# Gate by chunk inside the scans, shared PSUM tiles in the second token block, and the output projection's loads between its weights

## The chip, the cores and the metric

The kernel runs on one core of a Trainium2 chip. The metric is the device time of one execution in microseconds. A core has five engines with queues of their own, each worked off in order: TensorE (PE, with its weight loads as PEld), VectorE (DVE), ScalarE (ACT), GpSimd (POOL) and SyncE (SP), whose queue issues most DMAs. ACT issues a few.

## What is computed

One layer of a diffusion backbone for 256 prompt tokens and 1024 sample tokens, width 1024, all in fp32. Cut to what matters here:

```python
h = rmsnorm(x, g_norm1) * (1.0 + scale_m) + shift_m
hc, gb, gc, z, xbc, dtf, dtb = jnp.split(h @ w_in, offs, axis=-1)
out_a = gb * dwconv1d(gc * hc, w_conv_short)
xbc = jax.nn.silu(dwconv1d(xbc, w_conv_ssd, b_conv_ssd))
y = y_f + y_b_rev[:, ::-1] + xh * d_skip[:, None]          # two scans, chunks of 128
y = rmsnorm(y * jax.nn.silu(z), g_ssd_norm)                # the gate, over 512 channels
x = x + gate_m * (jnp.concatenate([out_a, y], axis=-1) @ w_out)
h2 = rmsnorm(x, g_norm2) * (1.0 + scale_f) + shift_f
u = dwconv(h2 @ w_up)                                      # 3x3 on the sample, width 3 on the prompt
ug, uv = jnp.split(u, 2, axis=-1)
x = x + gate_f * ((jax.nn.silu(ug) * uv) @ w_down)         # then a final rmsnorm
```

## The kernel before

Channels lie on the 128 partitions, tokens along the free dimension. A product in fp32 is made of three matmuls with rounded parts: `wload` brings a weight tile into `raw`, ACT rounds it to `whi`, DVE or POOL subtracts to `wlo`, and `mm3` runs `whi` x hi, `whi` x lo, `wlo` x hi for each of the k tiles. A framework schedules the program: it traces the instructions, orders them for each engine by their place in the program and by when they are ready in a model of time, and sets the semaphores. `high_priority` moves what stands in it ahead. `after(a, b)` adds an edge that only orders.

The stages in order: the modulation and the first norm; `xbc`, the input projections of the scan; the scans; the gate; the output projection `wout` and the second norm; the feed-forward part in two token blocks (A: the prompt and 8 rows of the grid, B: the other 8 rows, 512 tokens), each of 22 pairs of `up` tiles (gate and value) with `down` tiles of the group before between them; a last norm.

**The scans.** The scan has a first pass, backward over the chunks (`ssd_pass1`), which stores a state for each chunk, and a second, forward (`ssd_pass2`), which makes the outputs. The prompt has 2 chunks, the sample 8. In the second pass a chunk takes two steps, one for each group of heads. A step takes one filler (`fill`), runs `output` (the matmuls into `yp`, then DVE adds them onto X) and, two steps ahead, `prep` (DVE adds the mask, ACT takes eight exponentials, DVE multiplies into `wm` and `csb`). The fillers are half projections of 24 matmuls that keep TensorE busy: the z projections of the sample (`zproj_halves`, 2 for each of 4 tiles, 8 in all) and the short convolution (`outa`, 6 for each of 4 tiles, 24 in all). The first pass over the sample takes one filler for each two chunks, the second pass 2, 2, 1, 1 over the prompt and 1 for each of 16 steps over the sample. What is left of the list runs after the scans.

**z and X.** `zproj_halves` copies z out of PSUM and ACT's queue stores it to DRAM (`zd`). X holds the scan's input and then its output: `xall` for the prompt, four tiles "xs" for the sample. `outa` stores its result as hi and lo to DRAM (`oad`).

**The gate** (lines 792 to 820) comes after both scans. For each token set it loads z, takes silu, multiplies it into X, squares on ACT, adds the four squares on DVE, sums over the partitions with a matmul against `ones` (L223), takes Ln and Exp on ACT for the reciprocal root (L226, L228), multiplies by gain and root, and splits the result into hi (ACT, L815) and lo (DVE) in the tiles `mya` (block A) and `myb` (block B). Before Ln a preload (L213) sets a table that holds Ln and Exp both.

**The output projection.** It loads `moa` (8 tiles of `oad`), `x1` (8 tiles of x) and `mob` (8 tiles) and then, in `wout`, for each of 8 tiles m the weights, `mm3` over `mya` and `moa`, and DVE adds onto `x1[m]`.

**PSUM.** From the output projection on there are three tiles "acc" of two banks each (`pacc2`) and two "dn" of one (`pdn`). In block B an `up` tile has 512 columns and fills one bank of an acc tile; a `down` tile has two parts of 288 columns, each in a dn.

Of the kernel before, what the change touches and what calls it, by code (L numbers as in the profile page):

```python
# [13 lines left out]
P = 128  # L14
# [41 lines left out]
def body(nc, tc, A):  # L56
    cnt = [0]

    def T(pool, shape, tag, bufs, dt=F32):
        cnt[0] += 1  # L60
        return pool.tile(list(shape), dt, tag=tag, bufs=bufs, name=f"{tag}_{cnt[0]}")
# [14 lines left out]
    def tt(out, a, b, op, eng=None):  # L76
        (eng or V).tensor_tensor(out=out, in0=a, in1=b, op=op)  # L77
# [17 lines left out]
    def smv(n):  # L95
        a, b = SMO[n]
        return sm[:, a:b]
# [174 lines left out]
    modv = mod.rearrange("p (b k) v -> p b k v", k=KT)  # L272
    badav = smv("bada").rearrange("p (b k) -> p b k", k=KT)

    def ada_block(k):
        wa = [T(xy, [P, 4, 2 * P], "xs", 4) for _ in range(2)]
        for i in range(2):
            dma(wa[i], A["w_ad1"][k, i])
        pm = psa()
        for j in range(KT):  # L280
            q = 32 * (j % 4)
            nc.tensor.matmul(pm[q:q + 32, 0:2 * P], sc[:, j, :], wa[j // 4][:, j % 4, :],
                             start=j < 4, stop=j >= 4, skip_group_check=True, tile_position=(0, q))
        s = T(cv, [P, 2 * P], "cv", 4)
        act(s, pm[:, 0:2 * P], AF.Copy)
        tp = pst()
        for b in range(2):
            nc.tensor.transpose(tp[:, b * P:(b + 1) * P], s[:, b * P:(b + 1) * P], ident)
        V.tensor_reduce(out=modv[:, 0:2, k],
                        in_=tp[:, 0:2 * P].rearrange("p (b g v) -> p b v g", b=2, g=4)[:, :, 0:2, :],  # L290
                        axis=mybir.AxisListType.X, op=ALU.add)
        tt(modv[:, 0:2, k], modv[:, 0:2, k], badav[:, 0:2, k].unsqueeze(2).broadcast_to([P, 2, 2]),
           ALU.add)
        ts(aff[:, 0, k], modv[:, 1, k], 1.0, smv("g1")[:, k:k + 1], ALU.add, ALU.mult)
# [55 lines left out]
        sets.append(s)  # L350
    SP, SS = sets
    oad = T(dr, [4, 2, P, TT], "oad", 1)
    zd = T(dr, [4, P, TT], "zd", 1)

    last_mm, mid_mm = [], [None]

# [44 lines left out]
    def zproj_halves(s, j, lo_eng):  # L401
        g = proj_halves(s, 12 + j, lo_eng)
        next(g)
        yield
        pp = next(g)
        z = T(cv, [P, s.T], "xl", 2)
        act(z, pp, AF.Copy)
        nc.scalar.dma_start(zd[j, :, s.t0:s.t0 + s.T], z)
        yield

    def outa(s, j, lo_eng):
# [170 lines left out]
            dma(st[0], A["st"][:, 1])  # L582
        return [(copies, step, c) for c in range(s.nc - 1, -1, -1)]

    def ssd_pass2(s, fill):


        sf = [None]
# [35 lines left out]
        def prep(u, g):  # L624
            csb = csbs[2 * u.c + g]
            wm = T(sw[0], [P, 8, L], "wm", 2)
            tt(wm.rearrange("p (a h) l -> p a h l", a=2), csb.rearrange("p (a h) l -> p a h l", a=2),
               s.mask.unsqueeze(2).broadcast_to([P, 2, 4, L]), ALU.add)
            for a in range(2):
                for h in range(4):  # L630
                    r = 32 * a + 4 * g + h
                    act(wm[:, a * 4 + h, :], wm[:, a * 4 + h, :], AF.Exp,
                        bias=s.tok[:, u.c, 0, r:r + 1])
            act(csb, csb, AF.Exp)
            tt(wm[:, 0:4, :], wm[:, 0:4, :], wm[:, 4:8, :], ALU.add)
# [33 lines left out]
        for i in range(2 * s.nc):  # L669
            behind = fill(s, i)  # L670
            if i % 2 == 1 and i + 1 < 2 * s.nc:
                u.step(behind)
            output(*us[i], behind)
            load(i + 3)
            if i + 2 < 2 * s.nc:
                if i % 2 == 0:
                    u = front(i // 2 + 1)
                us.append((u, i % 2))
                prep(*us[-1])
        if s.name == "p":  # L680
            dma(A["o_stf"], sf[0])

# [8 lines left out]
    SP.B, SP.C = bcp[0:2], bcp[2:4]  # L691
    SS.hi = lambda k: hs_hi[k]
    SS.lo = lambda k: hs_lo[k]
    SS.X = [T(xy, [P, TS], "xs", 4) for _ in range(4)]
    d4_s = dtcopy(SS, pd_s)
    for i in range(N_LOOP):
        xbc(SS, i, SS.X[i], PG)
# [58 lines left out]

    def fill(s, i):

        for _ in range(2 if s.name == "p" and i < 2 else 1):
            next(filler)  # L760
        return mid_mm[0]

# [3 lines left out]
    def steps(cps, behind):  # L766
        for (step, c, cp), b in zip(cps, behind):
            step(c, cp, b)
# [6 lines left out]
    for i in range(0, len(scan), 2):  # L775
        cps = pairs(scan[i:i + 2])
        next(filler)
        steps(cps, (mid_mm[0], last_mm[-1]))
    ssd_pass2(SP, fill)
    ssd_pass2(SS, fill)  # L780
    for _ in filler:
        pass
    close_pool(g_sw)
# [2 lines left out]

    g_ya, ya = open_pool("ya")
    g_yb, yb = open_pool("yb")
    g_gt, gt_ = open_pool("gt")
    mya = [[T(ya, [P, TA], "ya", 8, F32R) for _ in range(2)] for _ in range(4)]  # L790
    myb = [[T(yb, [P, OA], "yb", 8, F32R) for _ in range(2)] for _ in range(4)]
    def gate(s, behind):
        n = s.T
        acc = T(gt_, [P, n], "gq", 3)
        for j in range(4):
            z = T(gt_, [P, n], "gz", 2)
            dma(z, zd[j, :, s.t0:s.t0 + n])
            act(z, z, AF.Silu)
            tt(s.X[j], s.X[j], z, ALU.mult)
            if j == 0:  # L800
                act(acc, s.X[j], AF.Square)
            else:
                q = T(gt_, [P, n], "gq", 3)
                sq = act(q, s.X[j], AF.Square)
                tt(acc, acc, q, ALU.add)
        r = T(gt_, [P, n], "gq", 3)
        rstd(r, acc, n, pst, 512, sq, behind)
        for j in range(4):
            y = s.X[j]
            stt(y, y, smv("gsd")[:, j:j + 1], r, ALU.mult, ALU.mult)  # L810
            parts = [(0, n, mya, s.t0)] if s.name == "p" else \
                [(0, TA - TP, mya, TP), (TA - TP, TS, myb, 0)]
            for a, b, dst, o in parts:
                hi = dst[j][0][:, o:o + b - a]
                act(hi, y[:, a:b], AF.Copy)  # L815
                tt(dst[j][1][:, o:o + b - a], y[:, a:b], hi.bitcast(F32), ALU.subtract)
    with tc.high_priority():
        gate(SP, last_mm[-5])
        gate(SS, last_mm[-3])
    close_pool(g_xy)  # L820

    close_pool(g_gt)
    close_pool(g_cv)
    close_pool(g_hs)
    close_pool(g_ps)
# [10 lines left out]
        for i in range(2):  # L836
            dma(moa[j][i].bitcast(F32), oad[j, i, :, 0:TA])
    x1 = [T(x1p, [P, TT], "x1", 8) for _ in range(KT)]
    for k in range(KT):
        dma(x1[k], xT[:, k, :])  # L840
    mob = [[T(ob, [P, TB], "ob", 8, F32R) for _ in range(2)] for _ in range(4)]
    for j in range(4):
        for i in range(2):
            dma(mob[j][i].bitcast(F32), oad[j, i, :, TA:TT])

    def pacc2():
        return T(ps, [P, 1024], "acc", 3)
# [10 lines left out]
    def wout(src, parts, t0):  # L858
        for m in range(KT):
            wh, wl = wload(A["w_out"][m], PV)  # L860
            pp = pacc2()
            outs = []
            for c, a, b, v in parts:
                outs.append((pp[:, c:c + b - a],
                             (lambda k, a=a, b=b: src[k][0][:, a:b]),
                             (lambda k, a=a, b=b: src[k][1][:, a:b])))
            mm3(outs, wh, wl, KT)
            for c, a, b, v in parts:
                xx = x1[m][:, t0 + a:t0 + b]
                stt(xx, pp[:, c:c + b - a], col(2, m, v), xx, ALU.mult, ALU.add)  # L870
# [50 lines left out]
    def norm2_b_steps():  # L921
# [6 lines left out]

        return norm2_steps(TA, TB, [(0, 0, TB, 1)], alloc, done)

    def up(blk, m, h2s):
        wh, wl = wload(A["w_up"][m], PG)
        pp = pacc2()
        parts = PARTS_A if blk == 0 else PARTS_B
        outs = []
        for c, a, b, v in parts:
# [60 lines left out]
    def down(blk, gi, gs, ms):  # L997
        nj = GROUPS[gi]
        j0 = sum(GROUPS[:gi])
        t0 = 0 if blk == 0 else OA  # L1000
        for m in ms:
            raw = T(ff, [P, 4, P], "draw", 2)[:, 0:nj]
            off = (j0 * KT + m * nj) * P * P
            dma(raw, A["w_down"][off:off + nj * P * P].rearrange("(p j c) -> p j c", p=P, j=nj))
            wh = T(ff, [P, 4, P], "dhi", 2, F32R)[:, 0:nj]
            act(wh, raw, AF.Copy)  # L1006
            wl = T(ff, [P, 4, P], "dlo", 2, F32R)[:, 0:nj]
            tt(wl, raw, wh.bitcast(F32), ALU.subtract, PG)
            for a, b, v in DPARTS[blk]:
                o = pdn()[:, 0:b - a]  # L1010
                mm3([(o, (lambda k: gs[k][0][:, a:b]), (lambda k: gs[k][1][:, a:b]))], wh, wl, nj)
                xx = x1[m][:, t0 + a:t0 + b]
                stt(xx, o, col(5, m, v), xx, ALU.mult, ALU.add)
# [199 lines left out]
```

## Time and profile before

| what | us |
|---|---|
| median of the runs (3: 1585.49 to 1588.96) | 1585.58 |
| the profiled execution | 1583.09 |
| its span, first to last instruction | 1581.3 |
| mean granted TensorE clock | 0.991 |
| TensorE busy | 1521.7 |
| DVE busy | 1104.5 |
| ACT busy | 645.9 |
| POOL busy | 513.3 |

A row of the timeline names the start, the duration, the engine, the line, the operation, what it writes and what it reads, its shape, how often it stands there in a row, and in brackets the idle time before it with what ended it. A group row of the waits names who waited for whom, the sum in us, the times and the longest. The start times count from the first instruction. In this execution the second scan of the sample lies at about 345 to 463 us, the gate between 463 and 513, the output projection of block A starts at 512, and block B runs from about 1160 us.

### The profile page before, as it was taken

The page shows a single profiled execution, that of the slowest core. Times are in us where ns is not written, and L with a number is a line of the kernel's source. Part 1 is how long each engine was busy: PE and PEld are TensorE (multiplying, and loading weights), DVE is VectorE, ACT ScalarE, POOL GpSimd, SP SyncE. Part 2 cuts the span into 40 slices and gives each one's busy share as a digit, 9 for nine tenths or more (in the row PEclk, how much of TensorE's full clock was granted, in tenths as well). Part 3 has the DMA queues.
Part 4 walks back from the last instruction along what each step waited for, and adds up shares of the span by engine and source line. Part 5 has one row for each costly group of instructions (what it writes and reads, how often), then busy time and mean ns, then how long its engine had stood idle before and what let it go on. Part 6 is the DMA issues. An engine that isn't in the chain of part 4 may idle for free. (4 is left out here: it accounts for less than half of the span.)

```text
span 1581.3 us, 22424 instructions
## 1 busy us (share of the span) xinstructions
PE 1521.7 (96%) x8692; PEld 1293.7 (82%) x8692; DVE 1104.5 (70%) x1629; ACT 645.9 (41%) x1004; POOL 513.3 (32%) x288
## 2 busy tenths in 40 slices
PE   6988999999997999999999999999999999999997
PEld 3688667888785788888888888898888888888886
DVE  5765626376857339797666598656679878798696
ACT  6553434356557125433333353332334433433333
POOL 1445001111110000433333333333346555445452
PEclk9999999999998999999999999999999999999999
DMA  8555554333323712322222233212253333343221
GB/s 303 213 187 167 209 207 153 126 128 133 127 106 126 298 64 84 100 74 81 65 66 65 72 131 109 79 59 75 72 184 99 102 96 100 107 160 97 93 79 61
DMA packets 81756, 191.98 MB, mean 121 GB/s; under 512 B 9298, under 2 KB 31474, under 8 KB 81650
## 3 DMA queue, kind: packets, MB, share of 16 engines
q1 hardware_dynamic: 79922, 187.41, 34.7%
q10 hardware_dynamic: 1728, 3.15, 0.5%
q8 instruction: 68, 1.11, 0.3%
q14 instruction: 38, 0.31, 0.1%
HBM read 167.37 MB, written 23.15 MB: 120 GB/s over the span
## 5 line engine op out<-in xcount | busy, mean ns | idle before, releaser
L80 DVE SCALAR_TENSOR_TENSOR cc<-acc,sm,cc 128x504 f32<-128x504 f32 (+5 forms) x836 | 546.2, 665 | 110.7 <-ACT cc L953 52.4
L77 POOL TENSOR_TENSOR wlo<-raw,whi 128x1024 fp32r<-128x1024 f32 (+2 forms) x83 | 192.6, 2321 | 680.1 <-ACT whi L151 418.9
L151 ACT ACTIVATE whi<-raw 128x1024 fp32r<-128x1024 f32 x90 | 95.1, 1057 | 215.7 <-PE acc L162 186.4
L80 DVE SCALAR_TENSOR_TENSOR x<-dn,mod,x 128x288 f32<-128x288 f32 (+2 forms) x176 | 96.3, 547 | 93.8 <-PE dn L164 93.3
L77 POOL TENSOR_TENSOR dlo<-draw,dhi 128x512 fp32r<-128x512 f32 (+1 forms) x88 | 108.8, 1237 | 88.5 <-ACT dhi L1006 88.4
L160 PE MATMUL acc<-ya,whi 128*128 128x512 f32 (+1 forms) x400 | 120.9, 360 | 11.5 <-ACT yb L815 8.4
L164 PE MATMUL acc<-ya,wlo 128*128 128x512 f32 (+1 forms) x400 | 120.6, 359 | 0.3 <-DVE wlo L77 0.3
L162 PE MATMUL acc<-ya,whi 128*128 128x512 f32 (+1 forms) x400 | 120.6, 359 | 0.0
L164 PE MATMUL acc<-oa,wlo 128*128 128x512 f32 (+1 forms) x400 | 119.0, 355 | 0.0
L162 PE MATMUL acc<-oa,whi 128*128 128x512 f32 (+1 forms) x400 | 118.8, 354 | 0.0
L160 PE MATMUL acc<-oa,whi 128*128 128x512 f32 (+1 forms) x400 | 118.3, 353 | 0.0
L160 PE MATMUL dn<-yb,dhi 128*128 128x288 f32 (+2 forms) x352 | 109.5, 311 | 5.3 <-DVE x L80 4.1
L77 POOL TENSOR_TENSOR wlx<-raw,whx 128x1024 fp32r<-128x1024 f32 (+2 forms) x32 | 74.0, 2312 | 119.3 <-ACT whx L151 104.6
L162 PE MATMUL dn<-yb,dhi 128*128 128x288 f32 (+2 forms) x352 | 109.0, 310 | 0.8 <-POOL yb L77 0.8
L164 PE MATMUL dn<-yb,dlo 128*128 128x288 f32 (+2 forms) x352 | 109.0, 310 | 0.0
L160 PE MATMUL acc<-h,whi 128*128 128x512 f32 x320 | 105.0, 407 | 1.2 <-ACT whi L151 1.2
L164 PE MATMUL acc<-h,wlo 128*128 128x512 f32 x320 | 100.8, 396 | 1.8 <-POOL wlo L77 1.8
L1006 ACT ACTIVATE dhi<-draw 128x512 fp32r<-128x512 f32 (+1 forms) x88 | 52.9, 602 | 120.6 <-PE dn L162 50.1
L162 PE MATMUL acc<-h,whi 128*128 128x512 f32 x320 | 101.6, 396 | 0.0
L160 PE MATMUL dn<-g,dhi 128*128 128x288 f32 (+2 forms) x304 | 95.2, 314 | 0.0
L162 PE MATMUL dn<-g,dhi 128*128 128x288 f32 (+2 forms) x304 | 94.8, 312 | 0.3 <-POOL g L77 0.3
L160 PEld LDWEIGHTS acc<-ya,whi 128*128 128x128 f32 x400 | 76.5, 192 | 22.6 <-ACT yb L815 8.8
(343 smaller groups left out, 3624.0 us busy)
## 6 DMA issues: line engine op xcount, KB each, us to landing
raw<-in_w_up SPq DMA_DIRECT2D x88, 512.0 KB, 3.2
x<-in_w_ada SPq DMA_DIRECT2D x32, 512.0 KB, 5.4
draw<-in_w_down SPq DMA_DIRECT2D x64, 256.0 KB, 2.6
x<-in_w_in SPq DMA_DIRECT2D x24, 512.0 KB, 3.4
raw<-in_w_in SPq DMA_DIRECT2D x22, 512.0 KB, 6.9
xs<-in_w_ad SPq DMA_DIRECT2D x16, 512.0 KB, 8.4
csb<-csds SPq DMA_DIRECT2D x16, 512.0 KB, 4.3
raw<-in_w_out SPq DMA_DIRECT2D x16, 512.0 KB, 3.3
```

The source lines that it names most:

```text
L77: (eng or V).tensor_tensor(out=out, in0=a, in1=b, op=op)
L80: V.scalar_tensor_tensor(out=out, in0=a, scalar=s, in1=b, op0=op0, op1=op1)
L151: act(hi, raw, AF.Copy)
L160: nc.tensor.matmul(o, wh[:, k, :], rh(k), start=k == 0, stop=False)
L162: nc.tensor.matmul(o, wh[:, k, :], rl(k), start=False, stop=False)
L164: mm = nc.tensor.matmul(o, wl[:, k, :], rh(k), start=False, stop=k == n - 1)
L1006: act(wh, raw, AF.Copy)
```

## The change

- The four tiles of X of the sample become one tile `xq`, of which `ada_block` uses quarters for its weights as it used the tiles before.
- `zd` is laid out by chunk. For the sample silu is taken as z leaves PSUM; the prompt's z is copied and gets its silu in the gate.
- The first pass over the sample takes two fillers for each two chunks, the second pass over the prompt 2, 1, 1, 1.
- `gate` is a generator of three parts: load z; multiply, square, add the squares of channels 0, 1 to those of 2, 3; two matmuls against `ones`, Ln, Exp, multiply by the root. It runs for the whole prompt and for each chunk of the sample, called behind the steps of the second pass by `post_p` and `post_s`. Its z is a tile "cv", of which there are four for this and for `outa`. There is no preload of a table. The last chunk's last part is behind the scan.
- Behind the scans the gain is multiplied as the tiles are split: ACT scales and rounds to hi, DVE makes lo.
- `wout` loads `x1[m]` and one tile of `mob` behind each weight tile, and the loads ahead of it are gone.
- In block B the gate and value tile of a pair share one acc tile, a bank each, and every odd `down` tile takes an acc tile for its two parts.

```diff
+    xq = T(xy, [P, 4, TS], "xs", 1)
-        wa = [T(xy, [P, 4, 2 * P], "xs", 4) for _ in range(2)]
+        wa = [xq[:, 2 * (k % 2) + i].rearrange("p (j c) -> p j c", j=4) for i in range(2)]
...
-    zd = T(dr, [4, P, TT], "zd", 1)
+    zd = T(dr, [TT // L, P, 4, L], "zd", 1)
...
-        act(z, pp, AF.Copy)
-        nc.scalar.dma_start(zd[j, :, s.t0:s.t0 + s.T], z)
+        act(z, pp, AF.Silu if s.name == "s" else AF.Copy)
+        nc.scalar.dma_start(zd[s.t0 // L:s.t0 // L + s.nc, :, j].rearrange("c p l -> p c l"),
+                            z.rearrange("p (c l) -> p c l", l=L))
...
                 prep(*us[-1])
+            post(i)
...
-        for _ in range(2 if s.name == "p" and i < 2 else 1):
+        for _ in range(2 if s.name == "p" and i == 0 else 1):
             next(filler)
...
         cps = pairs(scan[i:i + 2])
         next(filler)
-        steps(cps, (mid_mm[0], last_mm[-1]))
-    ssd_pass2(SP, fill)
-    ssd_pass2(SS, fill)
+        mid_mm[0] = last_mm[-1]
+        next(filler)
+        steps(cps, (last_mm[-2], last_mm[-1]))
+
+    def gate(x, c0, n):
+
+        z = T(cv, [P, 4, n], "cv", 4)
+        for c in range(n // L):
+            dma(z[:, :, c * L:(c + 1) * L], zd[c0 + c])
+        yield
+        if c0 == 0:
+            act(z, z, AF.Silu)
+        tt(x, x, z, ALU.mult)
+        act(z, x, AF.Square)
+        tt(z[:, 0:2], z[:, 0:2], z[:, 2:4], ALU.add)
+        yield
+        pp = psa()
+        for i in range(2):
+            mm = nc.tensor.matmul(pp[:, 0:n], ones, z[:, i], start=i == 0, stop=i == 1)
+            if i == 0:
+                after(mm, last_mm[-1])
+        r = z[:, 2]
+        act(r, pp[:, 0:n], AF.Ln, scale=1.0 / 512, bias=epsc)
+        act(r, r, AF.Exp, scale=-0.5)
+        tt(x, x, r.unsqueeze(1).broadcast_to([P, 4, n]), ALU.mult)
+        yield
+
+    gate_p = gate(xall, 0, TP)
+    gates = [gate(xq[:, :, c * L:(c + 1) * L], SP.nc + c, L) for c in range(SS.nc)]
+
+    def post_p(i):
+        if i == 2 * SP.nc - 1:
+            next(gate_p)
+
+    def post_s(i):
+
+        c = i // 2
+        if i == 0:
+            next(gate_p)
+            next(gates[0])
+        if i == 1:
+            next(gate_p)
+        if i % 2 == 1:
+            next(gates[c])
+        else:
+            if c > 0:
+                next(gates[c - 1])
+            if c + 1 < SS.nc:
+                next(gates[c + 1])
+
+    ssd_pass2(SP, fill, post_p)
+    ssd_pass2(SS, fill, post_s)
+    with tc.high_priority():
+        next(gates[-1])
     for _ in filler:
         pass
...
     with tc.high_priority():
-        gate(SP, last_mm[-5])
-        gate(SS, last_mm[-3])
+        for x, dst, o in ((xall, mya, 0), (xq[:, :, 0:TA - TP], mya, TP), (xq[:, :, TA - TP:], myb, 0)):
+            n = x.shape[2]
+            for j in range(4):
+                g = smv("gsd")[:, j:j + 1]
+                hi, lo = [t[:, o:o + n] for t in dst[j]]
+                act(hi, x[:, j], AF.Copy, scale=g)
+                stt(lo, x[:, j], g, hi.bitcast(F32), ALU.mult, ALU.subtract)
...
-    for k in range(KT):
-        dma(x1[k], xT[:, k, :])
...
-    for j in range(4):
-        for i in range(2):
-            dma(mob[j][i].bitcast(F32), oad[j, i, :, TA:TT])
...
             wh, wl = wload(A["w_out"][m], PV)
+            if t0 == 0:
+                dma(x1[m], xT[:, m, :])
+                dma(mob[m // 2][m % 2].bitcast(F32), oad[m // 2, m % 2, :, TA:TT])
...
-        pp = pacc2()
+        if blk == 0:
+            pp = pacc2()
+        elif m < N_FF:
+            pair[0] = pacc2()
+            pp = pair[0][:, 0:512]
+        else:
+            pp = pair[0][:, 512:1024]
...
-            for a, b, v in DPARTS[blk]:
-                o = pdn()[:, 0:b - a]
+            both = pacc2() if blk == 1 and m % 2 else None
+            for i, (a, b, v) in enumerate(DPARTS[blk]):
+                o = (pdn() if both is None else both[:, 512 * i:512 * i + 512])[:, 0:b - a]
```

More of the change, by code (lines that the diff above doesn't have):

```diff
@@ L583, in ssd_pass1, with ssd_pass2 @@
         return [(copies, step, c) for c in range(s.nc - 1, -1, -1)]
-    def ssd_pass2(s, fill):
+    def ssd_pass2(s, fill, post):
         sf = [None]
@@ L693, in body @@
     SS.lo = lambda k: hs_lo[k]
-    SS.X = [T(xy, [P, TS], "xs", 4) for _ in range(4)]
+    SS.X = [xq[:, i] for i in range(4)]
     d4_s = dtcopy(SS, pd_s)
@@ L788, in body @@
     g_yb, yb = open_pool("yb")
-    g_gt, gt_ = open_pool("gt")
     mya = [[T(ya, [P, TA], "ya", 8, F32R) for _ in range(2)] for _ in range(4)]
     myb = [[T(yb, [P, OA], "yb", 8, F32R) for _ in range(2)] for _ in range(4)]
-    def gate(s, behind):
-        n = s.T
-        acc = T(gt_, [P, n], "gq", 3)
-        for j in range(4):
[L796 to L816, printed above, removed]
-    with tc.high_priority():
-        gate(SP, last_mm[-5])
-        gate(SS, last_mm[-3])
+    with tc.high_priority():
+        for x, dst, o in ((xall, mya, 0), (xq[:, :, 0:TA - TP], mya, TP), (xq[:, :, TA - TP:], myb, 0)):
[5 more added lines that the diff above has]
+                stt(lo, x[:, j], g, hi.bitcast(F32), ALU.mult, ALU.subtract)
     close_pool(g_xy)
-    close_pool(g_gt)
     close_pool(g_cv)
@@ L838, in body @@
     x1 = [T(x1p, [P, TT], "x1", 8) for _ in range(KT)]
-    for k in range(KT):
-        dma(x1[k], xT[:, k, :])
     mob = [[T(ob, [P, TB], "ob", 8, F32R) for _ in range(2)] for _ in range(4)]
-    for j in range(4):
-        for i in range(2):
-            dma(mob[j][i].bitcast(F32), oad[j, i, :, TA:TT])
     def pacc2():
@@ L929, in norm2_b_steps @@
         return norm2_steps(TA, TB, [(0, 0, TB, 1)], alloc, done)
+    pair = [None]
     def up(blk, m, h2s):
         wh, wl = wload(A["w_up"][m], PG)
-        pp = pacc2()
+        if blk == 0:
[5 more added lines that the diff above has]
+            pp = pair[0][:, 512:1024]
         parts = PARTS_A if blk == 0 else PARTS_B
```

## The prediction

> **What bounds the kernel now.** I read the totals first, then busy time by stretches of the span, then TensorE's waits, then the timeline where they cluster.
>
> ```profile
> PE 1521.7 (96%) x8692; PEld 1293.7 (82%) x8692; DVE 1104.5 (70%) x1629; ACT 645.9 (41%) x1004; POOL 513.3 (32%) x288
> 320.00:480.00 160.00, 158.76 (x1007) 129.37 (x1006) 113.05 (x148) 91.17 (x195) 21.92 (x9) 1.00 0.34 119
> 480.00:560.00 80.00, 65.25 (x303) 53.16 (x302) 43.07 (x49) 31.06 (x39) 2.89 (x1) 0.89 0.57 210
> 1280.00:1320.00 40.00, 40.00 (x226) 35.71 (x225) 32.34 (x55) 14.00 (x20) 22.34 (x13) 1.00 0.31 96
> ```
>
> In the stretches the columns after the length are the busy time of PE, PEld, DVE, ACT and POOL, then granted clock, DMA share and GB/s. TensorE is the bound: 158.8 of 160 us in the second scan, all of a stretch of the second token block. The hole is between scans and output projection: 65.3 of 80 us, at a clock of 0.89. Who left TensorE waiting from 200 to 560 us:
>
> ```profile
> PE acc L160 <- ACT yb L815: 8.4, 1, 8.4
> PE acc L160 <- ACT whi L151: 4.3, 2, 3.1
> PE acc L164 <- POOL wlo L77: 1.8, 1, 1.8
> PE sa L532 <- DVE xd L77: 1.3, 1, 1.3
> PE acc L164 <- DVE wlo L77: 0.3, 1, 0.3
> ```
>
> 8.4 us are the gate itself: the first matmul of the output projection waits for the last split tile that `gate` writes. The waits for whi and wlo are weight conversions: one pair stands behind the gate's work on ACT, the other (3.1 us) is a weight of the output projection and begins on SP's queue:
>
> ```profile
> 518.50 6.99 SPq L840 DMA_DIRECT2D x<-in_xT  x8
> 530.18 27.11 SPq L149 DMA_DIRECT2D raw<-in_w_out  x6
> 541.97 0.84 ACT L880 ACTIVATE nq<-x 128x768 f32<-128x768 f32 x1 [7.62 <-DVE x L80]
> 542.72 1.99 ACT L151 ACTIVATE whi<-raw 128x1024 fp32r<-128x1024 f32 x2
> 543.81 0.62 PE L160 MATMUL acc<-ya,whi 128*128 128x256 f32 x2 [3.06 <-ACT whi L151]
> ```
>
> Eight loads of x1 are issued ahead of six weight loads. The late weights are converted on ACT only behind a square of x1, which itself waited 7.6 us for the tile before; so it is the load's place in the order that costs. Behind each hole TensorE also runs slowly:
>
> ```profile
> 512.47 0.98 PE L160 MATMUL acc<-ya,whi 128*128 128x256 f32 x2 [8.40 <-ACT yb L815]
> 518.34 0.52 PE L160 MATMUL acc<-ya,whi 128*128 128x256 f32 x2
> 518.70 0.52 PE L162 MATMUL acc<-ya,whi 128*128 128x256 f32 x2
> 545.07 0.61 PE L164 MATMUL acc<-ya,wlo 128*128 128x256 f32 x2 [0.29 <-DVE wlo L77]
> 549.16 0.52 PE L160 MATMUL acc<-ya,whi 128*128 128x256 f32 x2
> 490.78 0.86 PE L160 MATMUL acc<-h,whi 128*128 128x512 f32 x2
> 494.65 0.62 PE L164 MATMUL acc<-h,wlo 128*128 128x512 f32 x2
> 464.79 0.62 PE L160 MATMUL acc<-h,whi 128*128 128x512 f32 x2
> 470.29 0.62 PE L160 MATMUL acc<-h,whi 128*128 128x512 f32 x2
> ```
>
> A row pair of the output projection takes 0.36 us (518.34 to 518.70). The nine from 512.47 to 518.34 took 5.87 instead of 3.2: 2.7 lost. From 545.07 to 549.16 are seven pairs, 4.1 instead of 2.5: 1.6 lost. A pair of the input projection takes 0.46 us (twelve rows from 464.79 to 470.29, which is one half projection, **5.5 us**); the five pairs from 490.78 to 494.65 took 3.87 instead of 2.3: 1.6 lost. **The stage loses** 8.4 + 4.3 + 1.8 + 0.3 + 2.7 + 1.6 + 1.6 = **20.7 us**.
>
> **The change, part by part.** *The holes.* After the change the gate of each chunk runs inside the scan. What stays behind the last output is one chunk's gate and the splits into mya and myb, twelve on ACT and twelve on DVE. Unit rows:
>
> ```profile
> 508.49 0.61 ACT L815 ACTIVATE yb<-xs 128x512 fp32r<-128x512 f32 x1
> 487.08 0.40 ACT L815 ACTIVATE ya<-xp 128x256 fp32r<-128x256 f32 x1
> 512.24 0.69 DVE L77 TENSOR_TENSOR ya<-xs,ya 128x512 fp32r<-128x512 f32 x1
> 468.39 0.43 DVE L77 TENSOR_TENSOR gq<-gq,gq 128x256 f32<-128x256 f32 x1 [0.51 <-ACT gq L804]
> ```
>
> Splits: ACT 4 × 0.40 + 8 × 0.61 = 6.5 us, DVE 4 × 0.43 + 8 × 0.69 = 7.2 us. Fillers: the list has 32 half projections. Before, the scans use 4 + 6 + 16 and 6 are left; after, 8 + 5 + 16, so 3 are left: 16.5 us of matmuls behind the last output. They cover 6.5 and 7.2 us, a gate of 4.0 (below), and the remaining short-convolution work. Only the last split of outa, its store and its reload come after the cover; four of eight k steps of the first output tile need mya alone, some 12 × 0.36 = 4.3 us of matmuls, and three accumulators let further tiles begin. I leave **3 us** (0 to 6): the 1.8 of a POOL conversion, plus 1.2 for the reload. The loads one by one take the 3.1 us wait and its 1.6 of slow rows away, since a weight then waits for one x1 and one mob at most; if that failed, these 4.7 would stay. Net: −20.7 + 3 = **−17.7**.
>
> *More TensorE work.* The sum over channels goes through the ones matrix in two halves, so twice the columns.
>
> ```profile
> 474.41 0.59 PE L223 MATMUL yp<-gq,ones 128*128 128x256 f32 x2
> 474.65 0.82 PE L160 MATMUL acc<-h,whi 128*128 128x512 f32 x2
> 475.31 0.62 PE L162 MATMUL acc<-h,whi 128*128 128x512 f32 x2
> 448.43 0.74 PE L160 MATMUL acc<-h,whi 128*128 128x512 f32 x2
> 455.86 0.74 PE L160 MATMUL acc<-h,whi 128*128 128x512 f32 x2
> ```
>
> 256 columns move the next pairs from 474.41 to 475.31, 0.9 instead of 0.46: 0.44 us. Before: 256 + 1024 columns, 2.2 us; after 4.4. Eight small groups break the stream; the 0.74 against 0.62 in the first pair after a scan output is 0.12 each, up to 0.2 with the issue before it. **+3.8** (2.2 to 5).
>
> *The scan.* A step is 7.43 us (448.43 to 455.86), a chunk 14.86. Per chunk DVE is busy 113.05/160 of that, 10.5 us, and ACT 91.17/160, 8.5 us. The gate adds:
>
> ```profile
> 919.60 1.28 ACT L226 ACT_TABLE_LOAD   x1
> 921.60 1.28 ACT L228 ACT_TABLE_LOAD   x1
> 475.53 0.47 ACT L226 ACTIVATE gq<-yp,epsc 128x256 f32<-128x256 f32 x1
> 476.01 1.28 ACT L798 ACT_TABLE_LOAD   x1
> 479.68 0.42 ACT L228 ACTIVATE gq<-gq 128x256 f32<-128x256 f32 x1
> ```
>
> Without the explicit preload, Ln loads a table and Exp loads another (919.60, 921.60); I take two loads for each of nine gates. ACT per chunk: 2 × 1.28 + 0.61 (square) + at most 0.47 and 0.42 = 4.0; DVE 0.69 + 0.43 + 0.69 = 1.8. So ACT goes to 12.5 and DVE to 12.3 of 14.86, both under TensorE. Behind a late Ln on ACT stand the exponentials of the mask of two steps on; DVE waits for those, and TensorE's output for DVE. The wm tiles are prepared two steps ahead, which leaves the chain a chunk. The before has no such gate in a scan; bounds: nothing, if the spare 2.4 us of ACT and 2.6 of DVE absorb it (a gain is excluded, nothing is taken out of the second scan), and 4.0 × 9 = 36 if every gate's ACT time stood bare. The nearest row is the 1.3 us that TensorE waited for xd, a tile handed over late once; 0.5 per gate gives **+4** (0 to 12). The prompt's silu on ACT, a table load and back, lies in this. The z loads are new on SP's queue in the scan; one waits for a cv tile until an older gate or outa has let go of it, and behind it stand the csb three steps on and the next w_in. They have two steps of cover, and the DMA share of the scan is 0.34, so I take 0 for them and for the store of z in pieces of 128 tokens; without the cover it is a step's wait, in the 12.
>
> The Trainium skill ("ScalarE: Activation LUTs", What ACT_TABLE_LOAD costs) speaks against this part: a switch costs about 2.66 us, 1.28 for the load and 1.38 of drain. The trace disagrees: the Ln at 475.53 ends at 476.00, and the load starts at 476.01. By the rule ACT would have 8.5 + 4.0 + 2 × 1.38 = 15.3 us in a chunk of 14.86 and the sum would be some 3 us worse, as an estimate.
>
> *The first scan* over the sample gets two half projections per two chunks in place of one. The xd wait of 1.3 lies there and a second half covers it: **−1** (−1.3 to +2, as z's silu can alternate tables with the exponentials).
>
> *PSUM of the second block.* TensorE's longest wait from 1080 us on, and the stretch in which it falls:
>
> ```profile
> PE dn L160 <- DVE x L80: 1.4, 1, 1.4
> 1400.00:1440.00 40.00, 37.41 (x215) 33.23 (x214) 39.17 (x59) 12.15 (x17) 18.93 (x11) 1.00 0.39 128
> ```
>
> DVE is busy 39.2 of 40 us there, and TensorE waits 1.4 for a down tile's bank. More banks let DVE fall behind without stopping TensorE, so the 1.4 goes. A pair holds its tile through both convolutions and an odd down tile takes one of the same three, so a wait can come instead. **−1.4** (−2.6, all that TensorE lacks in that stretch, to +4, three new waits of that kind).
>
> **Sum:** −17.7 + 3.8 + 4 − 1 − 1.4 = **−12.3**. The profiled execution took 1583.1 us (span 1581.3 and 1.8 around it), so 1570.8; the median of the runs is 2.5 higher, 1585.6, which gives **1573.3**. Instructions of ada_block only change how their tile is named: 0.
>
> **Rivals.** A row of today's gate bears on the second of them:
>
> ```profile
> 498.99 0.69 ACT L226 ACTIVATE gq<-yp,epsc 128x512 f32<-128x512 f32 x1 [2.76 <-PE yp L223]
> ```
>
> 1. *The scan takes back most.* DVE and ACT work in order and wait for each other; at 83% each a gate can cost TensorE 1.5 us, 9 × 1.5 = 13.5 in place of 4. For it: each gate has one chain DVE, ACT, TensorE, ACT, DVE. Against: 1.2 us idle in 160 today. 1583.
> 2. *Slower: Ln holds ACT.* The ones matmul is tied behind the end of the newest half projection. If Ln stands at ACT's head while that half still runs, ACT stops for up to 5.5 us per gate: 8.5 + 4.0 + 5.5 = 18.0 against 14.86, and the scan runs at ACT's pace, 3.1 × 8 = 25 in place of 4. It decides once the wait passes 2.4 us. For it: in the row, ACT stands 2.8 us before the ones matmul. Against: the squares are ready a step earlier, so the matmul is early if Ln is placed after it. 1573.3 + 21 = 1594.
>
> 3. *The hole only shrinks.* The last chunk's gate, splits, convolution and weight conversions meet on DVE and ACT as they do now; 3 becomes 11.7 (half of the 8.4 wait, the 2.7 of slow rows and a second POOL wait of 1.8 more): 1582.
> 4. *The loads change nothing.* An x1 load waits for memory and holds the next weights on the in-order queue: the 4.7 stays, 1578.
>
> **Chances.** Forecast 0.62 (1565 to 1578), rival 1 0.12, rival 2 0.09, rival 3 0.07, rival 4 0.06, better than all this (no new stall, no hole, 1562) 0.04. A measurement of this kernel can tell 0.3%, 4.8 us. Faster by more than that (under 1580.8): forecast, rival 4, the better case and some of 1 and 3: 0.77. Within: 0.13. Slower: 0.10. The range leaves out rival 2 and the far better end: **1562 to 1585**.
>
> **What would show it.** Right: no wait of TensorE over 2 us between the last scan output and the second output tile; no rows at 0.65 us a pair there; 18 more table loads in the scan, with TensorE above 97% busy; no wait for a w_out weight. Wrong: a step longer than 7.9 us, with TensorE's output waiting for DVE's wm or csb (rival 1), or Ln waiting over 2.4 us for the ones matmul (rival 2); an output projection that starts after a gap for ya or oa (rival 3); new waits of the second block for a cc.

## The result and the profile after

The changed kernel takes 1646.98 us (median of 6 runs, 1639.9 to 1652.04); the kernel before, beside it, 1586.39 (6 runs, 1584.27 to 1591.11). The ratio is **1.0375** (95% interval 1.0344 to 1.0405): slower by some 60 us, where 12 us less were forecast and the range ended at 1585. The profiled execution took 1646.87 us. One execution of experiment 5 below took 2510.5 us at a granted clock of 0.557 (without it that experiment's median is 1578.91 us), and the ratios compare the others.

The page of the changed kernel, its first line and the totals:

```profile
span 1645.1 us, 22507 instructions
PE 1545.9 (94%) x8722; PEld 1308.5 (80%) x8722; DVE 1092.8 (66%) x1634; ACT 661.2 (40%) x1025; POOL 514.3 (31%) x288
```

TensorE has 30 matmuls more than before (8722 against 8692) and is busy for 24 us more, yet for a smaller share of the span; no other engine has grown by much. The same stretches as before the change, in the same columns, and then all of the second token block (block B):

```profile
320.00:480.00 160.00, 153.86 (x987) 124.49 (x986) 124.49 (x165) 114.50 (x228) 23.15 (x9) 1.00 0.39 131
480.00:560.00 80.00, 74.05 (x417) 62.15 (x416) 40.57 (x53) 33.88 (x48) 2.41 (x1) 1.00 0.54 200
1280.00:1320.00 40.00, 35.60 (x182) 30.39 (x183) 22.69 (x40) 10.03 (x14) 14.18 (x9) 0.92 0.18 60
1400.00:1440.00 40.00, 32.66 (x154) 26.90 (x153) 27.78 (x43) 15.57 (x21) 14.06 (x9) 0.87 0.39 138
1160.00:1645.00 485.00, 428.81 (x2234) 371.24 (x2234) 338.04 (x557) 156.71 (x227) 208.10 (x128) 0.94 0.26 85
```

The last row against the same work in the kernel before:

```profile
1165.00:1581.00 416.00, 402.99 (x2234) 356.54 (x2234) 346.45 (x557) 156.80 (x227) 207.78 (x128) 0.99 0.30 99
```

The second scan lost some 5 us of TensorE time (158.76 to 153.86), the hole behind it got back 9 (65.25 to 74.05, at full clock). Block B begins 5 us earlier, at 1160 in place of 1165, and then runs 485 us in place of 416, with the same 2234 matmuls, 557 instructions of DVE's and 227 of ACT's. Of these 69 us TensorE stands idle for 43.2 (485.00 − 428.81 against 416.00 − 402.99), and 25.8 are the same matmuls at a lower granted clock (428.81 − 402.99; 0.94 against 0.99). 69 − 5 is the whole difference of the two spans, 63.8. So the loss is block B's, and no engine has more to do there: it is waiting. TensorE's waits from 1160 us on, after the change:

```profile
PE acc L160 <- DVE cc L80: 23.9, 6, 5.9
PE dn L162 <- POOL yb L77: 5.6, 4, 2.8
PE dn L164 <- POOL dlo L77: 3.9, 3, 1.9
PE dn L160 <- ACT yb L1029: 3.6, 2, 2.3
PE acc L160 <- DVE x L80: 2.9, 5, 1.1
```

And in the kernel before, from 1165 us on:

```profile
PE dn L160 <- DVE x L80: 1.4, 1, 1.4
PE dn L160 <- ACT dhi L1006: 1.2, 1, 1.2
```

The new wait is the first matmul into an acc tile (L160) behind a tap of a convolution on DVE (L80, output cc). The longest of the six in the timeline of the changed kernel, rows left out between:

```profile
1262.51 2.30 DVE L80 SCALAR_TENSOR_TENSOR cc<-acc,sm,cc 128x504 f32<-128x504 f32 x3
...
1264.16 0.39 PE L164 MATMUL acc<-oa,wlo 128*128 128x512 f32 x1
1264.39 0.39 PE L160 MATMUL acc<-oa,whi 128*128 128x512 f32 x1
...
1272.58 1.32 ACT L1007 ACTIVATE cc<-acc,sm 128x448 f32<-128x448 f32 x2
...
1273.38 9.86 DVE L80 SCALAR_TENSOR_TENSOR cc<-acc,sm,cc 128x64 f32<-128x64 f32 x17 [8.57 <-ACT cc L1007]
...
1276.49 0.29 PE L164 MATMUL dn<-yb,dlo 128*128 128x288 f32 x1
...
1282.73 0.76 PE L160 MATMUL acc<-ya,whx 128*128 128x512 f32 x1 [5.95 <-DVE cc L80]
...
1283.16 0.75 DVE L77 TENSOR_TENSOR cc<-cc,cc 128x576 f32<-128x576 f32 x1
1283.30 0.63 PE L162 MATMUL acc<-ya,whx 128*128 128x512 f32 x1
1283.72 0.63 PE L164 MATMUL acc<-ya,wlx 128*128 128x512 f32 x1
1283.82 0.74 DVE L80 SCALAR_TENSOR_TENSOR cc<-acc,sm,cc 128x504 f32<-128x504 f32 x1
...
1284.60 0.68 ACT L1025 ACTIVATE cc<-cc 128x576 f32<-128x576 f32 x1
...
1284.71 0.77 PE L160 MATMUL acc<-ya,whi 128*128 128x512 f32 x1
```

The two engines take turns. From 1264.8 DVE has nothing: TensorE finishes two up tiles at nearly the same time, and ACT opens both from 1272.58 on. Then DVE has 17 taps in a row, TensorE runs out of down tiles at 1276.8, and its next up tile waits 5.95 us for one of those taps. When it may go on, its matmuls follow each other at 0.42 us (1283.30, 1283.72) where they stood at 0.23 before the wait (1264.16, 1264.39): the slow rows of the 25.8 us.

Two things can be read from these rows once each tile is followed through its weights, its read by ACT and its nine taps.

The matmul at 1282.73 is the first of a *new* pair, the gate of the eighth. The tap that let it go ended at 1282.59 and is the last one of the value tile of the sixth pair, whose product with its gate follows at 1283.16. So TensorE stood until a whole acc tile came free. All six waits are of this kind, each released by the last tap of a value tile: three are the gates of new pairs (5.95, 5.51 and 3.08 us), two are odd down tiles (5.44 and 1.16), one is a tile of the last `down` (2.72).

Why the acc tiles come free so late is seen one row on. At 1284.71 the value tile of the seventh pair begins, 0.15 us after the last tap of its own gate (1283.82 to 1284.56; the silu of the gate follows at 1284.60). The value tile of the same pair in the kernel before began while DVE was at its gate's taps, the last six of which are the second row:

```profile
1265.43 0.40 PE L160 MATMUL acc<-ya,whi 128*128 128x512 f32 x1
...
1266.16 4.57 DVE L80 SCALAR_TENSOR_TENSOR cc<-acc,sm,cc 128x441 f32<-128x441 f32 x6
```

It is so for every pair. After the change all 22 value tiles begin after their gate's last tap, 0.15 to 4.4 us behind its end; before, all 22 began 4.6 to 13.4 us ahead of it. A value tile starts 24.7 us after its gate on average, in place of 7.7, and from the gate's first matmul to the value's last tap a pair takes 40.3 us in place of 23.9, all of it in one of three acc tiles. The halves of a tile lie in different banks, and the kernel before, where each up tile has an acc tile to itself, has no such order. So the theory: **the framework keeps the order of uses by tile, not by bank, and the value half may not be written until the gate half has been read for the last time.** The rival is the prediction's own worry, that a pair *holds* its banks through both convolutions and too few are left.

### The profile page after: what moved, and what is told of

Read it like the earlier page. It is cut to its first block, busy times and chain, and to the rows that moved or that the text cites. A ratio compares the mean times of both kernels' runs of the same rounds, so it can differ in the third digit from the quotient of the medians.

```text
span 1645.1 us, 22507 instructions
## 1 busy us (share of the span) xinstructions
PE 1545.9 (94%) x8722; PEld 1308.5 (80%) x8722; DVE 1092.8 (66%) x1634; ACT 661.2 (40%) x1025; POOL 514.3 (31%) x288
## 5 line engine op out<-in xcount | busy, mean ns | idle before, releaser
L80 DVE SCALAR_TENSOR_TENSOR cc<-acc,sm,cc 128x504 f32<-128x504 f32 (+5 forms) x836 | 539.6, 665 | 140.1 <-ACT cc L1007 53.1
L80 DVE SCALAR_TENSOR_TENSOR x<-dn,mod,x 128x256 f32<-128x256 f32 (+2 forms) x136 | 75.6, 558 | 109.6 <-PE dn L164 109.5
L160 PE MATMUL acc<-ya,whi 128*128 128x512 f32 (+1 forms) x400 | 121.9, 363 | 10.9 <-DVE cc L80 8.6
L160 PE MATMUL acc<-oa,whi 128*128 128x512 f32 (+1 forms) x400 | 118.7, 354 | 0.0
L160 PE MATMUL acc<-h,whi 128*128 128x512 f32 x320 | 104.8, 404 | 0.0
L160 PEld LDWEIGHTS acc<-ya,whi 128*128 128x128 f32 x400 | 76.6, 192 | 23.6 <-issue 9.2
L160 PE MATMUL dn<-yb,dhi 128*128 128x256 f32 (+2 forms) x264 | 84.0, 321 | 7.0 <-ACT yb L1029 3.6
L162 PE MATMUL dn<-yb,dhi 128*128 128x256 f32 (+2 forms) x264 | 84.9, 322 | 5.6 <-POOL yb L77 5.6
L80 DVE SCALAR_TENSOR_TENSOR x<-acc,mod,x 128x288 f32<-128x288 f32 (+3 forms) x80 | 43.5, 555 | 67.6 <-PE acc L164 67.6
L164 PE MATMUL dn<-yb,dlo 128*128 128x256 f32 (+2 forms) x264 | 84.9, 323 | 2.5 <-POOL dlo L77 2.5
L164 PEld LDWEIGHTS acc<-ya,wlo 128*128 128x128 f32 x400 | 76.1, 190 | 13.0 <-POOL wlo L77 1.6
```

Source lines behind the costliest of these rows:

```text
L80: V.scalar_tensor_tensor(out=out, in0=a, scalar=s, in1=b, op0=op0, op1=op1)
L160: nc.tensor.matmul(o, wh[:, k, :], rh(k), start=k == 0, stop=False)
L162: nc.tensor.matmul(o, wh[:, k, :], rl(k), start=False, stop=False)
L164: mm = nc.tensor.matmul(o, wl[:, k, :], rh(k), start=False, stop=k == n - 1)
```

## The experiments

Each was run beside the kernel before, whose medians were 1584.9, 1585.83 and 1585.73 us in the three series (runs 1 to 4, 5 to 8, 9 to 12); 1% is 15.9 us. Beside the changed kernel it was 1586.39, so a difference between medians of two series carries up to 1.5 us of that.

**1. Gate and loads, without the PSUM edits.** The up tiles get an acc tile each, all down tiles go to dn:

```diff
-        if blk == 0:
-            pp = pacc2()
-        elif m < N_FF:
-            pair[0] = pacc2()
-            pp = pair[0][:, 0:512]
-        else:
-            pp = pair[0][:, 512:1024]
+        pp = pacc2()
...
-            both = pacc2() if blk == 1 and m % 2 else None
-            for i, (a, b, v) in enumerate(DPARTS[blk]):
-                o = (pdn() if both is None else both[:, 512 * i:512 * i + 512])[:, 0:b - a]
+            for a, b, v in DPARTS[blk]:
+                o = pdn()[:, 0:b - a]
```

> The changed kernel without its two PSUM edits: the gate by chunk and the loads one by one stay. Theory 1 (two banks of one tile are tied: the value tile's first matmul waits until the gate tile's convolution has read the other bank) and theory 2 (odd down tiles take the acc tiles that the pairs need) both put the whole loss of 61 us in the second block: 1574 us, with TensorE busy 40 of 40 us from 1240 to 1400 us. Theory 3 (the gate or the loads shifted the order of all that follows) expects 1630 us or more.

Measured: 1581.21 us, ratio 0.998 (0.9971 to 0.999).

**2. The PSUM edits alone**, in the kernel before (the lines of experiment 1 the other way round).

> The kernel before with the two PSUM edits alone. Theories 1 and 2: some 70 us slower than before, 1655 us, since the gate and the loads had taken some 10 back. Theory 3: no change, 1586 us.

Measured: 1655.26 us, ratio 1.0447 (1.0426 to 1.0468). The two PSUM edits make the loss by themselves, with or without the rest.

**3. Of the PSUM edits only the pair in one acc tile**; gate and loads as changed, all down tiles in dn (the second part of the diff of experiment 1).

> The changed kernel with pairs sharing a tile, but all down tiles in dn. Theory 1: most of the loss stays, 1625 to 1650 us, with waits of TensorE's first acc matmul for DVE's cc. Theory 2: the loss goes, under 1585 us.

Measured: 1628.73 us, ratio 1.0279 (1.0259 to 1.03). All 22 value tiles begin after their gate's last tap here too, and a pair takes 40.5 us. TensorE's waits for an acc tile behind a tap (acc L160 for DVE's cc) add up to only 7.4 us from 1160 us on, against 23.9 in the changed kernel, so the loss is not the sum of these waits.

**4. Of the PSUM edits only the odd down tiles in an acc tile**; gate and loads as changed (the first part of that diff).

> The changed kernel with odd down tiles in an acc tile, but each up tile in an acc tile of its own. Theory 1: a small loss, since the second part of an odd down tile waits only for one addition of 0.5 us on the first part: 1575 to 1590 us. Theory 2: most of the loss stays, over 1610 us.

Measured: 1585.05 us, ratio 1.0004 (0.9991 to 1.0017). Above experiment 1 the pairs cost 47.5 us, the down tiles 3.8, and both together 1646.98 − 1581.21 = 65.8: more than the sum. The tie shows in the down tiles as well: here all 20 second parts begin after the addition of the first, and TensorE's wait for it (acc L160 for DVE's x) is 3.8 us in five times; in experiment 7, where each part has a tile, all 20 begin before it. That the odd down tiles compete with the pairs for acc tiles would explain the rest: two of the six waits above are theirs, 6.6 us. No run takes that apart.

**5. The loads alone**: `x1[m]` and `mob` behind the weights of `wout` in the kernel before.

> The kernel before with the loads one by one alone. If the wait of 3.1 us for whi and the 1.6 of slow rows behind it go: 4.7 less, 1580 us. If the loads are hidden or collide elsewhere: 1585 us.

Measured: 1579.53 us, ratio 0.9961 (0.9952 to 0.9971).

**6. The gate alone**: as experiment 1, with the loads ahead of `wout` again.

> The kernel before with the gate by chunk alone. The hole behind the scans (some 16 us with its slow rows) goes and 12 come back in the scan, as ones matmuls that wait for the squares and 3.5 us of more matmuls: 1582 to 1586 us. If the gate in the scan were nearly free, 1574 us.

Measured: 1583.91 us, ratio 0.9996 (0.9981 to 1.0011). The gate inside the scans, which was to bring most, brings nothing that can be told. TensorE's waits from 200 to 560 us in this kernel, the two longest:

```profile
PE sa L800 <- DVE cv L77: 6.4, 4, 3.2
PE acc L160 <- ACT whi L151: 3.1, 1, 3.1
```

The second is the late weight of the output projection. In experiment 1, with the loads one by one, it is not among the waits any more. The first, L800, is the matmul against `ones` of the gate, and it is new; below.

**7. The same banks as tiles of one bank each.** Six acc tiles of 512 columns in place of three of 1024; a pair takes two, an odd down tile two, and an up tile of block A and a tile of `wout` one for each part:

```diff
-        return T(ps, [P, 1024], "acc", 3)
+        return T(ps, [P, 512], "acc", 6)
...
-        pp = pacc2()
+        pps = [pacc2() for _ in parts]
...
-                o = pdn()[:, 0:b - a]
+                o = (pacc2() if blk == 1 and m % 2 else pdn())[:, 0:b - a]
```

> The changed kernel with six acc tiles of one bank in place of three of two: every up tile of the second block has a tile of its own, odd down tiles take two, and each other user of a two-bank tile takes two of one bank. The same banks serve the same work as in the change; only the tie between two banks of a tile is gone. Theory 1 (the tie costs): 1575 to 1582 us, as the kernel without the PSUM edits (1581) or a little better. Theory 2 (the way the banks are shared out costs): over 1610 us.

Measured: 1570.23 us, ratio 0.9904 (0.9886 to 0.9923). The same six banks and the same two users, and the loss of 65.8 us has become a gain of 11.0. All 22 value tiles begin 5.3 us or more ahead of their gate's last tap again. The stretch of block B in which TensorE lacked 2.6 us in the kernel before (1400 to 1440 there) lies some 8 us earlier here:

```profile
1392.00:1432.00 40.00, 40.00 (x228) 35.81 (x227) 39.37 (x61) 12.66 (x18) 18.88 (x11) 1.00 0.43 141
```

TensorE is busy all the time beside a DVE that is at 39.4 of 40 us: that is what the banks were for.

**8. The gate's third part one step later**, in the kernel of experiment 1: the matmuls against `ones`, Ln, Exp and the root of a chunk go behind the second step of the next chunk in place of its first, and the load of a chunk's z goes one step later with them:

```diff
         if i % 2 == 1:
-            next(gates[c])
-        else:
             if c > 0:
                 next(gates[c - 1])
+            next(gates[c])
             if c + 1 < SS.nc:
                 next(gates[c + 1])
```

> Gate by chunk and loads one by one as in the change, no PSUM edits, and the last part of each chunk's gate one step later, so that the squares are done well before TensorE comes to the ones matmul. If the scan loses its time to that wait on TensorE (6.4 us and the slow rows behind it, in the kernel without the PSUM edits): 4 to 8 us less than it, 1574 to 1577 us. If the loss is the table loads on ACT: no change, 1581 us.

Measured: 1572.94 us, ratio 0.9925 (0.9905 to 0.9944): 8.3 us less than experiment 1. What went is seen in the timeline of experiment 1, at one gate:

```profile
375.74 2.38 POOL L77 TENSOR_TENSOR wlo<-raw,whi 128x1024 fp32r<-128x1024 f32 x1 [12.35 <-ACT whi L151]
376.18 3.01 DVE L77 TENSOR_TENSOR xp<-xp,cv 128x1024 f32<-128x1024 f32 x1
...
379.12 0.68 DVE L77 TENSOR_TENSOR xs<-xs,cv 128x512 f32<-128x512 f32 x1
379.72 0.59 DVE L80 SCALAR_TENSOR_TENSOR xs<-xs,sm,yp 128x128 f32<-128x128 f32 x2
379.83 0.63 ACT L795 ACTIVATE cv<-xs 128x512 f32<-128x512 f32 x1 [3.26 <-DVE xs L77]
380.23 0.68 DVE L77 TENSOR_TENSOR xd<-sa,toks 128x512 f32<-128x512 f32 x1
380.83 0.41 DVE L77 TENSOR_TENSOR cv<-cv 128x256 f32<-128x256 f32 x1
...
381.39 1.19 PE L800 MATMUL sa<-cv,ones 128*128 128x128 f32 x4 [3.19 <-DVE cv L77]
381.56 1.28 ACT L804 ACT_TABLE_LOAD   x1
382.86 0.37 ACT L804 ACTIVATE cv<-sa,epsc 128x128 f32<-128x128 f32 x1
383.24 1.28 ACT L805 ACT_TABLE_LOAD   x1
```

TensorE has come to the matmul against `ones` and works in order; the matmul needs the sum of squares (`cv<-cv`, 380.83), that needs the square on ACT, that the product `xs<-xs,cv`, and that stood behind a DVE operation of 3.01 us. So TensorE stood for 3.19 us with the matmuls of a half projection behind it in its queue. A step later the sum has long been made. The waits from 200 to 560 us in experiment 8:

```profile
PE sa L535 <- DVE xd L77: 2.5, 2, 1.3
PE acc L160 <- DVE cv L77: 1.4, 1, 1.4
PE sa L800 <- DVE cv L77: 1.4, 1, 1.4
```

L800 is down from 6.4 us to 1.4, and the scan is full, with 13 of the gate's 17 table loads in this stretch:

```profile
320.00:480.00 160.00, 159.31 (x1032) 130.07 (x1031) 129.74 (x171) 120.31 (x240) 23.91 (x9) 1.00 0.40 132
```

**9. One-bank tiles for the up tiles alone**; all down tiles in dn (experiment 7 without its last line).

> As the kernel with six one-bank accumulators (1570.2), but all down tiles of the second block in the two dn tiles. If the gain over the kernel without the PSUM edits (11.0 us) is that of up tiles that come free one bank at a time, most of it stays: 1570 to 1573. If it is that of the odd down tiles having other banks than the even ones, the wait of dn for DVE's x is back (4.1 us in sum and the slow rows behind it) and the time is 1577 to 1581.

Measured: 1574.49 us, ratio 0.9932 (0.9918 to 0.9945). It lies between the two: of the 11.0 us some 6.7 are the up tiles' (and `wout`'s), which in block A give their banks back one at a time and in block B have six tiles in place of three, and 4.3 the down tiles'.

**10. The two repairs together**, experiments 7 and 8.

> Gate in the scans with its part of sum and root one step later, the loads one by one, six accumulators of one bank. If the two repairs touch different stretches (the scan, 8.3 us of medians; the second token block, 11.0 us), their gains add: 1581.2 - 8.3 - 11.0 = 1561.9, a span near 1559, TensorE's wait at L800 at most 1.4 us in sum, no wait of a dn or acc of over 1 us for DVE's x in the second block. If the time that one repair saves is only waited for elsewhere (DVE, busy nearly all of the second block, becomes the bound), at most the larger gain is left: about 1570.

Measured: **1560.87 us** (5 runs, 1559.98 to 1562.75), ratio 0.9846 (0.9833 to 0.986). The gains add (1561.9 were to come out by their sum). It is faster than both kernels of this case:

```profile
span 1558.7 us, 22521 instructions
PE 1515.0 (97%) x8722; PEld 1293.1 (83%) x8722; DVE 1087.7 (70%) x1634; ACT 661.0 (42%) x1025; POOL 513.5 (33%) x288
```

The same 8722 matmuls as in the changed kernel take 31 us less of TensorE's time.

**11. One-bank tiles in the kernel before**, gate and loads untouched.

> The kernel before with six one-bank accumulators, odd down tiles of the second block taking two of them; gate and loads as before. If the gain of separate banks stands by itself it is the 11 us seen on top of gate and loads: 1585.8 - 11 = 1575 (1573 to 1578). If it needs the other two edits (it fills holes that they moved), the time stays at 1583 to 1586.

Measured: 1574.4 us, ratio 0.9933 (0.9918 to 0.9948). 1585.73 − 1574.4 = 11.3: the gain of the banks does not hang on the other edits. In the two profiled executions it lies in both blocks: from ACT's first read of an up tile in block A to its first in block B are 523.1 us before and 519.3 here, from there to the end 415.0 and 409.4.

**12. One-bank tiles, but the gate's bank held as long as the value's**, in experiment 7:

```diff
             tap(o[:, 0:RB, :GW - 1], u[:, :, 1:], 8)
+            if m < N_FF:
+                held[0] = pp
+            else:
+                tt(T(ff, [P, 1], "hold", 2), held[0][:, 0:1], cc[:, 0:1], ALU.add)
```

> As the kernel with six one-bank accumulators, but an added DVE operation of one column, behind the last tap of a value tile, reads the gate tile's bank, so a pair holds both banks through both convolutions as the shared tile does; nothing uses its result. The matmuls of the value tile have nothing to wait for in the gate's taps. If the loss of the change came of a wait between the two banks of one tile, this kernel stays near 1570.2 plus 22 short operations of some 0.1 us: 1571 to 1576. If it came of a pair holding its banks too long (as the prediction has it), the loss comes with it: 1600 and over, with TensorE idle for acc tiles in the second block.

Measured: 1568.8 us, ratio 0.99 (0.9881 to 0.9919). The added operation stands 22 times in the trace, behind the last tap of each value tile, and takes 0.15 to 0.16 us; it reads the gate's bank, so the bank is held until then. Nothing is lost. TensorE's waits in its block B, from 1145 us on, are these three:

```profile
PE dn L1109 <- DVE oa L77: 1.3, 1, 1.3
PE dn L162 <- POOL yb L77: 0.8, 1, 0.8
PE dn L1109 <- ACT oa L1098: 0.2, 1, 0.2
```

The rival falls as a cause of its own: six banks are enough for pairs that hold the gate's bank to the end. A pair takes 23.8 us here, though, against 40.3 in the changed kernel, and that difference is the tie's, since the value tiles begin ahead of the gate's last tap again. So the tie comes first, and the long holding, with TensorE's waits for a free tile, follows from it. Experiments 3 and 12 differ in whether the two banks are one tile or two. They also differ in where the odd down tiles lie (4.3 us by experiment 9), in the one-bank tiles of block A and `wout`, and in that a shared tile takes the value's bank already with the gate's first matmul, where here it is taken when the value tile begins, 7.7 us later; the last of these was not tried by itself. How much the tie costs by waits and how much by the order in which TensorE's work then runs was not taken apart.

## Why the prediction was wrong, step by step

- **PSUM of the second block, −1.4 (−2.6 to +4): the step that failed.** It came out at +65.8 on top of the other edits (experiment 1 against the changed kernel) and, alone, at a ratio of 1.0447, which is +71 (experiment 2). The step expected that a pair might hold its tile too long and priced that at "three new waits of that kind". Waits for a free acc tile did come, six of 23.9 us in sum, but not for the reason given: experiment 12 shows that holding through both convolutions costs nothing while a pair takes 24 us. What the step didn't look for was an order between the two halves of one tile. That changes when each value tile may *begin*, 22 times, and stretches a pair to 40 us; in place of three waits, TensorE stood idle for 43.2 us more and ran 25.8 us longer at a lower clock. There was a sign of it before the run: the diff puts a half that is being read and a half that is being written into one tile, and the framework sets the waits. The upper end of the range was worked out from the nearest wait in the trace, that of a down tile for one addition.
- **The gain that the step expected was there, and larger.** "More banks let DVE fall behind without stopping TensorE" holds once the banks are tiles of their own: −11 to −12 in place of −1.4 (experiments 7, 10, 11). The step had read TensorE's waits from 1080 us on only; up tiles of two parts in block A, too, give their banks back one by one in these kernels, and over the whole span of the kernel before the wait for a dn is larger, with 2.7 of it in block A:

```profile
PE dn L160 <- DVE x L80: 4.1, 2, 2.7
```

- **The scan, +4 (0 to 12): right in kind, too small, and for another reason.** Experiment 8 gives 8.3 us back. The text expected wm and csb to come late, or Ln to stop ACT at its head (rival 2). Ln did not wait: at 382.86 it follows its table load at once. It was TensorE that stopped at its own head, because "the squares are ready a step earlier" did not hold: the product that the squares need waits in DVE's queue. That is the chain of rival 1 (DVE, ACT, TensorE), which was priced at 13.5. Of the 18 table loads that were forecast 17 are there (nine at L804, eight at L805), and no cost of them shows: experiment 8 has 13 in a stretch with TensorE busy for 159.3 of 160 us.
- **The holes, −20.7 + 3 left.** From 470 to 570 us TensorE still waits, in experiment 1, for these:

```profile
PE sa L800 <- DVE cv L77: 3.2, 3, 1.3
PE acc L160 <- DVE cv L77: 1.4, 1, 1.4
PE acc L162 <- DMA oa<-oad: 0.3, 1, 0.3
```

  4.9 us where 3 (0 to 6) were left, 3.2 of it the gate's own chain at L800; the waits for yb (8.4), for wlo (1.8) and the clock of 0.89 are gone. Of this the loads were to take 4.7. They took 2.7 on top of the gate (1583.91 to 1581.21) and, alone, 0.39%, 6.2 us: their mechanism is as told, their price between the two.
- **More TensorE work, +3.8: right in size.** The time from the start of each matmul against `ones` to TensorE's next start adds up to 4.73 us in experiment 1 and to 1.26 in the kernel before: +3.5. By this count the two sums behind the term, 2.2 and 6.0, were each about 1 us too high, and that the two errors cancel is luck.
- **The first scan, −1 (−1.3 to +2): wrong sign, inside its bounds.** The wait for xd was to be covered; in experiments 1 and 8 there are two of 1.3 in place of one.

Without the PSUM term the sum was −17.7 + 3.8 + 4 − 1 = −10.9. Experiment 1 gives −3.2 (0.2% of 1585.6), experiment 8, which takes the scan's stalls away, −11.9.

## What to carry to other kernels

When two values that live at different times are put into one tile to save space, ask first in what unit the framework orders accesses: a half that is still being read can hold back the half that is to be written, and the tile is then held for longer as well. With a tile for each bank the same saving cost nothing here. When a dependent matmul is moved into the stream of a full TensorE, place it where its operand is ready by a whole step, counting the queue of the engine that makes the operand, since an in-order engine pays for a short wait with all that stands behind it.

## What the runs showed of the hardware

**TensorE after a wait.** Behind the wait of 5.95 us the matmuls of 512 columns started 0.42 us apart, and 0.23 before it. The Trainium skill ("TensorE: Matmul & The Clock Gate", Part 1) states that the clock falls to half after an idle window of some 3.4 us and gives 426.7 and 215.7 ns for 512 columns; the trace agrees for this wait. It doesn't show 3.4 us as a threshold: behind the wait of 3.08 us at 1508.74 the matmuls started 0.43 us apart too, and behind one of 2.72 us at 1611.24 those of 320 columns 0.27 us apart, against 0.15 later. In block B 43.2 us of idle time came with 25.8 us of slow matmuls.

**DVE beside GpSimd.** The operation of 3.01 us in the timeline shown with experiment 8, which is of experiment 1's kernel, took 1.21 us earlier in that kernel. There is a second long one there, a product into wm that alone takes 1.21 to 1.23 us:

```profile
353.15 1.21 DVE L77 TENSOR_TENSOR xp<-xp,cv 128x1024 f32<-128x1024 f32 x1
...
360.98 2.41 POOL L77 TENSOR_TENSOR wlo<-raw,whi 128x1024 fp32r<-128x1024 f32 x1 [16.70 <-ACT whi L151]
...
361.47 3.00 DVE L77 TENSOR_TENSOR wm<-csb,sm 128x1024 f32<-128x1024 f32 x1
```

Both long ones began while a subtraction on POOL ran, and both ended 1.07 to 1.08 us after it: 360.98 + 2.41 = 363.39 and 364.47, 375.74 + 2.38 = 378.12 and 379.19. So the DVE operation did nearly nothing until POOL was done. The Trainium skill ("SBUF — State Buffer", Who interferes with whom) states that a DVE instruction with two SBUF inputs contends with a GpSimd instruction that reads SBUF, and calls the ports that they share an exclusive lock; the trace agrees. At this gate one weight conversion on POOL, 2.4 us long, thus made the squares late and TensorE stand.
